# Spreading the reciprocal softmax sums over partitions: TensorE transposes against VectorE blocks and DRAM transfers

## The chip, the cores and the metric

The kernel runs on one core of one Trainium2 chip. The metric is the device time of one launch in microseconds (us); for each kernel it is the median of a few runs. Everything else in this text comes from one execution that the hardware profiler recorded.

A core has these engines: TensorE (in the profile PE for matmuls, PEld for the loads of their weights), VectorE (DVE), ScalarE (ACT), GpSimd (POOL), and SyncE (SP), which here only issues transfers. Each engine works through its own queue in order.

## The reference

Two layers of a hybrid decoder. Each layer takes 528 positions (16 learned meta tokens and 512 real ones) of width 1024. One projection feeds eight heads of attention with a forget gate and four heads of retention; their outputs go through one output projection, and a SwiGLU network follows. The part that the change touches is the softmax of the attention heads:

```python
def attend(q_blk, c_q, q_pos, k_, v_, c_k, k_pos):
    s = jnp.einsum('bhqd,bhkd->bhqk', q_blk, k_).astype(jnp.float32) * scale
    s = s + c_q[..., :, None] - c_k[..., None, :]
    s = jnp.where(k_pos[None, :] <= q_pos[:, None], s, -jnp.inf)
    p = jax.nn.softmax(s, axis=-1)
    return jnp.einsum('bhqk,bhkd->bhqd', p.astype(v_.dtype), v_)
```

Every query row is divided by the sum of its exponentials. All arithmetic is float32.

## The kernel before

Activations are kept transposed: features lie on the 128 partitions and positions along the free axis. Every matmul that matters is run three times, on a high and a low part of each operand (`split`: ScalarE casts the high part, VectorE subtracts it to get the low one).

Attention heads go in pairs: head pair g (0 to 3) holds heads 2g and 2g+1, called s = 0 and 1, of 64 features each. For each s and each block b of 128 queries the steps are:

- `scores(s, b)`: TensorE multiplies queries and keys (line 497), VectorE adds the mask to the diagonal (503) and the gates and takes the maximum (504), ScalarE takes the exponential and its sum over the keys (517). Queries lie on partitions here, so the sum is one column of 128 numbers.
- `turn(s, b)`, three steps later: TensorE transposes the unnormalised probabilities block by block (`transpose_into`, line 409), ScalarE and VectorE split them into `pth` and `ptl` (lines 137 and 138). The last 16 columns of all four blocks are transposed by VectorE in 32 by 32 blocks (line 521, tile `pe`).
- `product(s)`: TensorE multiplies values and probabilities (line 567); ScalarE copies one half of the result (570, tile `ol`) and VectorE adds the other (571). Features now lie on partitions and queries along the free axis.

The division is put off to the end of the pair. After the last `scores` the eight columns of sums (two heads, four blocks) are turned into reciprocals (line 525). ScalarE spreads each of them over 64 columns (527). In `product(1)` TensorE transposes the four 128 by 128 blocks so made (576), which leaves in PSUM, for each feature row, the reciprocal of its head and query, and VectorE multiplies the product of the pair by it (577). Then the pair is split (`mix_tile`) for the output projection, which comes much later for most pairs.

The four retention heads are worked on in the same stretch: `scores` (694, 699), `product` (724), `head_norm`, `gate`. They share ScalarE, VectorE and the four one-bank PSUM tiles (`psum_a`) with attention. Between these steps TensorE runs the dense projections (`dense_steps`, line 210), whose weights SyncE loads from DRAM (line 153, tile `raw`, three buffers), ScalarE casts (186) and, for most, GpSimd subtracts (187).

The order on TensorE is written out by hand: `merge` and `spread` place the steps between the chunks of the dense projections, and `manual_schedule` keeps that order. On the other engines a scheduler decides the order when the program is built, from its own estimates of durations. So an edit on one engine can move neighbouring instructions on others, although their lines are the same.

`tags` gives the tile `tq` a ring of four buffers (tag `w`) that several helpers share; the spread reciprocals take one of them.

Of the kernel before, what the change touches and what calls it, by code (L numbers as in the profile page):

```python
# [10 lines left out]
F32 = mybir.dt.float32  # L11
# [6 lines left out]
SEQ = 512  # L18
META = 16
T = SEQ + META  # L20
# [10 lines left out]
NBLK = SEQ // 128  # L31
# [8 lines left out]
def hybrid_kernel(ctx, tc, x_t, w_in, w_fl, w_out, w_gate, w_up, w_down, vecs, b_fg, rope, decay, mask, ident, out_t):  # L40
    nc = tc.nc

    const = ctx.enter_context(tc.tile_pool(name="const", bufs=1))
    state = ctx.enter_context(tc.tile_pool(name="state", bufs=1))
# [8 lines left out]
    idt = const.tile([128, 128], F32, name="idt")  # L53
# [10 lines left out]
    onec = const.tile([128, 1], F32, name="onec")  # L64
    nc.vector.memset(onec, 1.0)

    p_tiles, t_tiles, pm_tiles, v_tiles, end_tiles, low_keys = [], [], [], [], [], []
    rot = {"pm": 0}

# [182 lines left out]
    def psum_a():  # L252
        return psa.tile([128, 512], F32, name="psa", tag="psa")
# [5 lines left out]
    def tt(name, dt=F32):  # L259
        tag, bufs = tags[name]  # L260
        return tmp.tile([128, T], dt, name=name, tag=tag, bufs=bufs)
# [198 lines left out]
    def fox_steps(g, st, ly, real):  # L460

        blocks = list(range(0 if real else -1, NBLK))
        todo = [(s, b) for s in range(2) for b in blocks]
        info = {}

        def values():
            st["v"] = [at(f"vv{s}", shape=(128, 5, 128)) for s in range(2)]
            for j0, n, p3 in transpose_into(st["vt"], KOFF):
                for s in range(2):
                    v = st["v"][s][:, j0:j0 + n]  # L470
                    a0, a1 = ROWS[s]
                    b0, b1 = ROWS[1 - s]
                    nc.scalar.copy(v[:, :, a0:a1], p3[:, :, a0:a1])
                    nc.vector.tensor_sub(v[:, :, b0:b1], p3[:, :, a0:a1], v[:, :, a0:a1].bitcast(F32))
            st["mt"] = at("mixt", F32)

        def span(b):
            nq = META if b < 0 else 128
            nk = META if b < 0 else META + 128 * (b + 1)
            return nq, nk, (0 if b < 0 else META + 128 * b)  # L480

        def scores(s, b):
            nq, nk, q0 = span(b)
            if b == blocks[0]:
                bc = at("bc", F32, bufs=2)
                hd = 2 * g + s
                nc.sync.dma_start(bc, ly["cdr"][hd:hd + 1, :].partition_broadcast(128))
                st["bc"] = bc
            bc = st["bc"]
            segs = FULL if nk == T else ((0, nk),)  # L490
            pt = take(pm_tiles, "pm") if b < 0 else p_tiles[0][:, PSTEP * b:PSTEP * b + nk]
            mins = []
            normalise()
            for c0, c1 in segs:
                sc = psum_a()
                for i, kk in enumerate(st["k"][s]):
                    nc.tensor.matmul(sc[0:nq, 0:c1 - c0], st["q"][s][:, q0:q0 + nq], kk[:, c0:c1],  # L497
                                     start=(i == 0), stop=(i == 1))
                nm = tmp.tile([128, 1], F32, name="nmax", tag="nmax", bufs=6)
                with tc.high_priority():  # L500
                    if c1 == nk:
                        diag = sc[0:nq, c1 - c0 - nq:c1 - c0]
                        nc.vector.tensor_add(diag, diag, msk[0:nq, 0:nq])
                    nc.vector.tensor_tensor_reduce(pt[0:nq, c0:c1], sc[0:nq, 0:c1 - c0], bc[0:nq, c0:c1],  # L504
                                                   -1.0, 3.0e38, ALU.add, ALU.min, nm[0:nq])
                mins.append(nm)
            nmax = mins[0]
            if len(mins) > 1:
                nc.vector.tensor_tensor(nmax, mins[0], mins[1], ALU.min)
            if b < 0:  # L510
                rsum = tmp.tile([META, 1], F32, name="rsum", tag="rsum", bufs=4)
            else:
                if (s, b) == (0, 0):
                    st["sums"] = tmp.tile([128, NBLK, 2], F32, name="sums", tag="sums")
                rsum = st["sums"][:, b, s:s + 1]
            pr = pt[0:nq, 0:nk]
            nc.scalar.activation(pr, pr, AF.Exp, bias=nmax[0:nq], scale=-1.0, accum_out=rsum)  # L517
            info[s, b] = pt
            if b == blocks[-1]:
                st["ends"] = at("pe", F32, (32, NBLK, 32), 2)  # L520
                nc.vector.transpose(st["ends"], ends(p_tiles[0])[96:128])
            if b < 0:
                info["open"] = (pr, rsum)
            elif (s, b) == todo[-1]:
                nc.vector.reciprocal(st["sums"], st["sums"])
                st["rows"] = tt("tq")
                nc.scalar.copy(st["rows"][:, 0:SEQ].rearrange("p (b s d) -> p b s d", b=NBLK, s=2),
                               st["sums"].unsqueeze(3).broadcast_to([128, NBLK, 2, 64]))

        def normalise():  # L530
            if "open" in info:
                pr, rs = info.pop("open")
                nc.vector.reciprocal(rs, rs)
                nc.vector.tensor_scalar_mul(pr, pr, rs)

        def turn(s, b):
            nq, nk, q0 = span(b)
            pth, ptl = t_tiles
            if (s, b) == todo[-2]:
                normalise()  # L540
            if b < 0:
                e = at("pe", F32, (32, NBLK, 32), 2)[:, 0]
                nc.vector.transpose(e, info[s, b])
                split(pth[0:META, 0, 0:META], ptl[0:META, 0, 0:META], e[0:META, 0:META])
                return
            for j0, n, p3 in transpose_into(info[s, b], [128 * j for j in range(b + 1)]):
                split(pth[:, j0:j0 + n, q0:q0 + nq], ptl[:, j0:j0 + n, q0:q0 + nq], p3[:, :, 0:nq])
            if b == blocks[-1]:
                split(*[corners(t)[0:META, 1:] for t in (pth, ptl)], st["ends"][0:META, :, 32 - META:32])

        def product(s):
            mt, v, pt = st["mt"], st["v"][s], t_tiles
            a0, a1 = ROWS[s]
            b0, b1 = ROWS[1 - s]
            ol = tt("ol")
            if not real:
                po = psum_a()
                for i, pp in enumerate(pt):
                    nc.tensor.matmul(po[:, 0:META], v[:, 0, :], pp[:, 0, 0:META], start=(i == 0), stop=(i == 1))
                with tc.high_priority():  # L560
                    nc.scalar.copy(ol[a0:a1, 0:META], po[b0:b1, 0:META])
                    nc.vector.tensor_add(mt[a0:a1, 0:META], po[a0:a1, 0:META], ol[a0:a1, 0:META])
            po = psum_a()
            for j in range(5):
                c0 = max(0, KOFF[j] - META)
                for i, pp in enumerate(pt):
                    nc.tensor.matmul(po[:, c0:SEQ], v[:, j, :], pp[:, j, META + c0:T],  # L567
                                     start=(j == 0 and i == 0), stop=(j == 4 and i == 1))
            with tc.high_priority():
                nc.scalar.copy(ol[a0:a1, META:T], po[b0:b1, :])  # L570
                nc.vector.tensor_add(mt[a0:a1, META:T], po[a0:a1, :], ol[a0:a1, META:T])
            if s == 1:

                rb = psum_a()
                for b in range(NBLK):
                    nc.tensor.transpose(rb[:, 128 * b:128 * b + 128], st["rows"][:, 128 * b:128 * b + 128], idt)
                nc.vector.tensor_mul(mt[:, META:T], rb, mt[:, META:T])
                mh, ml = mix_tile(2 * (g % 2))
                split(sv(mh, real), sv(ml, real), sv(mt, real))
                st["mix"] = (mh, ml)  # L580

        steps = []
        n = len(todo)
        lag = 3
        for i in range(n + lag):
            if i < n:
                steps.append(lambda a=todo[i]: scores(*a))
            if i == 1:
                steps.append(values)
            if i >= lag:  # L590
                s, b = todo[i - lag]
                if s == 1 and b == blocks[0]:
                    steps.append(late(lambda: product(0)))
                steps.append(lambda a=(s, b): turn(*a))
        steps.append(lambda: product(1))
        cut = len(steps) - lag - 1
        return steps[:cut], steps[cut:]
# [627 lines left out]
    def layer(l):  # L1225

        real = l == DEPTH - 1
        QC = REAL if real else FULL
        ly, ff = {"wait": []}, {}
        fox = [{} for _ in range(FP)]  # L1230
        ret = [{} for _ in range(RH)]

# [170 lines left out]
```

## Time and profile before

| what | value |
|---|---|
| time, median of 3 runs | 1278.95 us (1278.76 to 1279.9) |
| time of the profiled execution | 1278.89 us |
| its span from the first to the last instruction | 1277.1 us |
| mean granted TensorE clock | 0.996 of full speed |
| PE busy | 1258.0 us, 99% |
| DVE busy | 1019.4 us, 80% |
| ACT busy | 687.7 us, 54% |
| POOL busy | 181.0 us, 14% |

The profiled execution is 1.8 us longer than its span, and 0.06 us from the median. In rows of a timeline the first number is the start and the second the duration, both in us; a bracket gives the idle time before it and what ended it. In rows of the chain of waits the same two numbers stand before the engine and line. A query on one line gives the shortest, median and longest duration in ns.

### The profile page before, as it was taken

To read this page: it belongs to the slowest core of one execution; us is meant where nothing else is said; L and a number is where in the kernel's file an instruction comes from. 1 tells how busy PE (TensorE), PEld (TensorE's weight loads), DVE (VectorE), ACT (ScalarE), POOL (GpSimd) and SP (SyncE) were. 2 spreads that over 40 slices of the span, in tenths; PEclk is the share of its full clock that TensorE was granted. 3 is DMA by queue.
4 is the path that set the end of the run, shared out by engine and by line. 5 is a ranking of instruction groups with operands and counts; after the bars stand their busy time and mean duration, and the time that the engine had idled before them with its cause. 6 is when DMAs were issued, how large, how long until landed. Compare 5 with 4: busy or idle time off the path is not lost.

```text
span 1277.1 us, 23190 instructions
## 1 busy us (share of the span) xinstructions
PE 1258.0 (99%) x9265; PEld 1197.8 (94%) x9265; DVE 1019.4 (80%) x1849; ACT 687.7 (54%) x1250; POOL 181.0 (14%) x150
## 2 busy tenths in 40 slices
PE   9999999999999999999999999999999999999997
PEld 8899999999999999999999989999789999999996
DVE  7888866879988888887687878568899878888867
ACT  7566655576544444444455665456764444444445
POOL 2233333210000000000014334332000000000001
PEclk9999999999999999999999999999999999999998
DMA  6222222223323333332323122222223333333321
GB/s 233 76 67 84 75 84 84 66 73 115 107 97 100 100 100 100 100 100 83 100 76 112 65 100 84 77 91 66 100 83 130 102 100 100 100 100 100 103 79 67
DMA packets 45677, 120.55 MB, mean 94 GB/s; under 512 B 5360, under 2 KB 12272, under 8 KB 45568
## 3 DMA queue, kind: packets, MB, share of 16 engines
q1 hardware_dynamic: 45136, 118.77, 28.4%
q8 instruction: 73, 1.20, 0.4%
q10 hardware_dynamic: 432, 0.29, 0.1%
q14 instruction: 36, 0.29, 0.1%
HBM read 116.91 MB, written 2.13 MB: 93 GB/s over the span
## 4 chain that ended last, share of the span: by engine, by line
PE 84%; DVE 10%; ACT 4%; DMA 1%; issue 1%; DVEq 0%; POOL 0%; ACTq 0%
PE psd L210 24%; PE psa L875 18%; PE psd L1010 14%; PE psd L875 13%; PE psa L1010 4%; PE psa L210 3%; PE psa L409 2%; PE psa L497 1%; PE psa L567 1%; PE psa L724 1%; PE psa L694 1%; DVE qs L429 1%; DMA bc<-cdr 1%; DVE pr L504 1%; DVE rsl L138 0%
## 5 line engine op out<-in xcount | busy, mean ns | idle before, releaser
L187 POOL TENSOR_TENSOR wlo<-raw,whi 128x512 fp32r<-128x512 f32 x126 | 172.3, 1381 | 380.2 <-ACT whi L186 380.2
L210 PE MATMUL psd<-xh,whi 128*128 128x264 f32 (+1 forms) x792 | 195.8, 315 | 0.0
L210 PE MATMUL psd<-xl,whi 128*128 128x264 f32 (+1 forms) x792 | 186.5, 303 | 0.6 <-DVE xl L313 0.6
L210 PE MATMUL psd<-xh,wlo 128*128 128x264 f32 (+1 forms) x792 | 186.9, 303 | 0.0
L210 PEld LDWEIGHTS psd<-xh,whi 128*128 128x128 f32 x792 | 128.7, 190 | 4.7 <-ACT whi L186 0.4
L210 PEld LDWEIGHTS psd<-xh,wlo 128*128 128x128 f32 x792 | 127.2, 188 | 6.2 <-DVE wlo L187 0.4
L210 PEld LDWEIGHTS psd<-xl,whi 128*128 128x128 f32 x792 | 128.0, 189 | 5.2 <-DVE xl L313 1.2
L186 ACT CAST whi<-raw 128x512 fp32r<-128x512 f32 (+1 forms) x168 | 98.3, 613 | 39.2 <-PE psd L210 19.9
L863 ACT CAST whi<-raw 128x1024 fp32r<-128x1024 f32 (+2 forms) x62 | 54.9, 885 | 51.3 <-PE psd L875 39.9
L863 ACT CAST fwhi<-raw 128x1024 fp32r<-128x1024 f32 (+2 forms) x62 | 55.6, 897 | 48.1 <-PE psd L875 40.5
L864 DVE TENSOR_TENSOR wlo<-raw,whi 128x1024 fp32r<-128x1024 f32 (+2 forms) x62 | 62.9, 1014 | 13.7 <-ACT whi L863 13.6
L864 DVE TENSOR_TENSOR fwlo<-raw,fwhi 128x1024 fp32r<-128x1024 f32 (+2 forms) x62 | 64.0, 1032 | 10.8 <-ACT fwhi L863 10.5
L875 PE MATMUL psa<-th,whi 128*128 128x264 f32 (+1 forms) x232 | 65.4, 282 | 0.0
L875 PE MATMUL psa<-th,wlo 128*128 128x264 f32 (+1 forms) x232 | 65.4, 282 | 0.0
L875 PE MATMUL psa<-tl,whi 128*128 128x264 f32 (+1 forms) x232 | 65.3, 282 | 0.0
L875 PE MATMUL psa<-th,fwhi 128*128 128x264 f32 (+1 forms) x224 | 63.4, 283 | 0.0
L875 PE MATMUL psa<-tl,fwhi 128*128 128x264 f32 (+1 forms) x224 | 63.3, 283 | 0.0
L875 PE MATMUL psa<-th,fwlo 128*128 128x264 f32 (+1 forms) x224 | 63.3, 282 | 0.0
L517 ACT ACTIVATE pr<-pr,nmax 128x144 f32<-128x144 f32 (+1 forms) x64 | 36.9, 576 | 42.8 <-DVE nmax L504 30.5
L941 ACT COPY e<-psa 128x264 f32<-128x264 f32 (+1 forms) x114 | 42.9, 376 | 27.9 <-PE psa L875 23.6
L863 ACT CAST fwhi<-S 128x1024 fp32r<-128x1024 f32 x20 | 21.0, 1049 | 68.6 <-PE psa L875 66.5
L1010 PE MATMUL psd<-ah,fwlo 128*128 128x264 f32 (+1 forms) x200 | 56.6, 330 | 0.0
(355 smaller groups left out, 4008.6 us busy)
## 6 DMA issues: line engine op xcount, KB each, us to landing
raw<-w_in SPq DMA_DIRECT2D x54, 512.0 KB, 3.5
raw<-w_gate SPq DMA_DIRECT2D x44, 512.0 KB, 4.0
fraw<-w_up SPq DMA_DIRECT2D x38, 512.0 KB, 3.4
raw<-w_down SPq DMA_DIRECT2D x64, 256.0 KB, 2.7
raw<-w_out SPq DMA_DIRECT2D x16, 512.0 KB, 3.5
raw<-w_down SPq DMA_DIRECT2D x32, 192.0 KB, 2.5
bc<-cdr SPq DMA_DIRECT2D x16, 264.0 KB, 3.3
raw<-w_up SPq DMA_DIRECT2D x6, 512.0 KB, 3.5
```

The source lines that it names most:

```text
L186: pin(nc.scalar.copy(hi, job["raw"][:, c0:c1]), pinned)
L187: pin(sub(lo, job["raw"][:, c0:c1], hi.bitcast(F32)), pinned)
L210: nc.tensor.matmul(ps[1][b][:, 0:c1 - c0], w[:, wk, :], x[:, c0:c1], start=(k == 0 and i == 0), stop=(k == n - 1 and i == 2))
L409: nc.tensor.transpose(ps[:, 128 * j:128 * j + 128], src[:, o:o + 128], idt)
L429: nc.vector.tensor_sub(sv(t, real, b0, b1), sv(tq, real, a0, a1), sv(t, real, a0, a1).bitcast(F32))
L497: nc.tensor.matmul(sc[0:nq, 0:c1 - c0], st["q"][s][:, q0:q0 + nq], kk[:, c0:c1], start=(i == 0), stop=(i == 1))
L517: nc.scalar.activation(pr, pr, AF.Exp, bias=nmax[0:nq], scale=-1.0, accum_out=rsum)
L863: nc.scalar.copy(hi, src)
L864: nc.vector.tensor_sub(lo, src, hi.bitcast(F32))
L875: nc.tensor.matmul(bank()[:, 0:b.shape[-1]], a[:, o + k, :], b, start=(fresh and k == 0 and i == 0), stop=(k == n - 1 and i == 2), skip_gr ...
L941: nc.scalar.copy(self.t["e"][:, i], self.t["x"][:, 0:w])
L1010: nc.tensor.matmul(v[:, 0:c1 - c0], a[:, s * n + k, :], b[:, c0:c1], start=(k == 0 and i == 0), stop=(k == n - 1 and i == 2))
```

## The change

The sums of a pair go into a fixed tile of 32 columns (two such tiles take turns), zeroed once. When all eight columns are there, VectorE takes the reciprocals and turns the tile in 32 by 32 blocks. Four small transfers write the eight useful rows of each block to DRAM, as eight rows of 128 numbers; two transfers read them back, each as one row of 512 numbers copied to 64 partitions. The last product of the pair reads this tile in SBUF in place of the one in PSUM. ScalarE's spreading copy and TensorE's four transposes are gone. The reciprocal and the turning are marked as of high priority for the scheduler. Lines below the second hunk have numbers higher by up to 9 in the changed kernel than in the diff's left side (577 becomes 582).

```diff
+    sum_tiles = [state.tile([128, 32], F32, name=f"sums{i}") for i in range(2)]
+    for t in sum_tiles:
+        nc.gpsimd.memset(t, 0.0)
...
             else:
-                if (s, b) == (0, 0):
-                    st["sums"] = tmp.tile([128, NBLK, 2], F32, name="sums", tag="sums")
-                rsum = st["sums"][:, b, s:s + 1]
+                rsum = sum_tiles[g % 2][:, NBLK * s + b:NBLK * s + b + 1]
...
             elif (s, b) == todo[-1]:
-                nc.vector.reciprocal(st["sums"], st["sums"])
-                st["rows"] = tt("tq")
-                nc.scalar.copy(st["rows"][:, 0:SEQ].rearrange("p (b s d) -> p b s d", b=NBLK, s=2),
-                               st["sums"].unsqueeze(3).broadcast_to([128, NBLK, 2, 64]))
+                sums = sum_tiles[g % 2]
+                turned = tmp.tile([128, 32], F32, name="turned", tag="turned")
+                with tc.high_priority():
+                    nc.vector.reciprocal(sums[:, 0:2 * NBLK], sums[:, 0:2 * NBLK])
+                    nc.vector.transpose(turned, sums)
+                rdr = tc.dram_tile([2 * NBLK, 128], F32, name=f"rdr{ly['l']}{g}")
+                for a in range(4):
+                    nc.sync.dma_start(rdr[:, 32 * a:32 * a + 32], turned[32 * a:32 * a + 2 * NBLK, :])
+                st["rows"] = tt("tq")[:, 0:SEQ]
+                wide = rdr.rearrange("(s b) q -> s (b q)", s=2)
+                for i, (a0, a1) in enumerate(ROWS):
+                    nc.sync.dma_start(st["rows"][a0:a1], wide[i:i + 1, :].partition_broadcast(64))
...
             if s == 1:
-
-                rb = psum_a()
-                for b in range(NBLK):
-                    nc.tensor.transpose(rb[:, 128 * b:128 * b + 128], st["rows"][:, 128 * b:128 * b + 128], idt)
-                nc.vector.tensor_mul(mt[:, META:T], rb, mt[:, META:T])
+                nc.vector.tensor_mul(mt[:, META:T], st["rows"], mt[:, META:T])
...
-        ly, ff = {"wait": []}, {}
+        ly, ff = {"wait": [], "l": l}, {}
```

## The prediction

> **What bounds the kernel now.** I read the page first: busy time per engine, then the chain that ended last.
>
> ```profile
> PE 1258.0 (99%) x9265; PEld 1197.8 (94%) x9265; DVE 1019.4 (80%) x1849; ACT 687.7 (54%) x1250; POOL 181.0 (14%) x150
> ...
> PE 84%; DVE 10%; ACT 4%; DMA 1%; issue 1%; DVEq 0%; POOL 0%; ACTq 0%
> ```
>
> TensorE is busy 99% of the span and carries 84% of the chain: time taken from it is time saved, if the work that feeds it keeps its places. The other 16% says that this isn't so everywhere. The timeline of TensorE, read for its idle time, shows where:
>
> ```profile
> 95.41 0.78 PE L409 MATMUL psa<-idt,pd 128*128 128x128 f32 x4 [0.88 <-DVE pd L449]
> 157.60 0.51 PE L210 MATMUL psd<-mxh,whi 128*128 128x264 f32 x2 [0.90 <-DVE h L778]
> ```
>
> Here TensorE waits 0.88 and 0.90 us for VectorE: in layer 0's first two pairs VectorE sets the end, and a TensorE saving is lost there. All times below are in us; each of the eight pairs (four a layer, g0 to g3) is costed by itself, since each has other neighbours.
>
> **What goes from TensorE.** The chain of waits around the removed transposes of one pair, and the group of the removed copies:
>
> ```profile
> 177.33 1.56 PE psd L210 x12
> ...
> 190.83 0.51 PE psa L576 x4
> 191.34 4.37 PE psd L210 x36
> ```
>
> ```profile
> L527 ACT COPY tq<-sums x8: 619/620/631, 67.7 to 873.6; 128x512 f32<-128x512 f32 x8
> ```
>
> The four transposes take 0.51. Twelve projection matmuls take 1.56 in the first row (it follows a product) and 4.37/3 = 1.46 in the row behind the transposes: what follows a product starts some 0.10 slower, and the transposes bear that now. So a pair saves 0.51 − 0.10 = 0.41 on TensorE, all eight at most 3.3. ScalarE loses eight copies of 0.62; it is 54% busy, so by itself this is worth nothing. What it does to the order comes below.
>
> **What is added, and whether it arrives in time.**
>
> ```profile
> 41.47 0.19 DVE L543 STREAM_TRANSPOSE pe<-pm 32x32 f32<-32x32 f32 x1
> 182.06 0.20 DVE L525 RECIPROCAL sums<-sums 128x8 f32<-128x8 f32 x1
> 193.15 0.69 DVE L577 TENSOR_TENSOR mixt<-psa,mixt 128x512 f32<-128x512 f32 x1
> ```
>
> ```profile
> bc<-cdr SPq DMA_DIRECT2D x16, 264.0 KB, 3.3
> ```
>
> ```profile
> 34.57 1.48 DMA cdr<-z
> ...
> 673.99 3.03 DMA cdr<-z
> ```
>
> The turn of 128x32 has no row; the nearest is a 32x32 turn of 0.19, and I take 0.2 (bounds 0.19 and 0.69, the multiply of 16 times the columns). The copy to rows in DRAM and back already occurs once a layer for the gates: `cdr` is written in 1.48 or 3.03, and its broadcast lands in 3.3. From the reciprocal: 0.4 on VectorE, four stores issued one after the other (estimate 0.4 each, half of the next row), 1.5 to 3.0 to land, two broadcasts issued, 3.3 to land:
>
> ```profile
> 36.06 0.81 SPq L487 DMA_DIRECT2D bc<-cdr  x2
> ```
>
> 0.4 + 1.6 + (1.5 to 3.0) + 0.8 + 3.3 = 7.6 to 9.1. The multiply comes 193.15 − 182.06 = 11.1 after the reciprocal in the tightest pair (layer 0, g2). So the rows arrive 2 to 3.5 before they are needed, and I charge nothing. SyncE's queue is passed by six transfers a pair; in six pairs the builder put one weight load between the stores and the broadcasts, which then starts some 2 early or late, with three `raw` buffers as cover: zero. If that cover fails, one late load of 512 KB costs at most the broadcasts' wait, about 3. The two memsets run before anything needs them.
>
> **What moves: the order on ScalarE and VectorE.** This is the large term. The changed program, as built, keeps TensorE's order but for the transposes, while around each place the scheduler has put ScalarE's and VectorE's neighbours in another order. In those stretches TensorE alternates between attention and retention, and both engines hand it operands with little slack. I followed the new order through the rows of before, pair by pair.
>
> *Layer 0, g0.*
>
> ```profile
> 69.95 0.49 PE L409 MATMUL psa<-idt,pr 128*128 128x128 f32 x3
> 70.32 0.71 DVE L138 TENSOR_TENSOR rsl<-sd,rsh 128x528 fp32r<-128x528 f32 x1 [0.73 <-ACT rsh L137]
> 71.24 0.40 PE L724 MATMUL psa<-rsl,rvh 128*128 128x512 f32 x1
> 71.98 0.48 ACT L137 CAST pth<-psa 128x384 fp32r<-128x384 f32 x1
> 73.40 0.59 ACT L137 CAST pth<-psa 128x512 fp32r<-128x512 f32 x1 [0.87 <-PE psa L409]
> ```
>
> `rsl` ends at 71.03 and TensorE uses it at 71.24. As built, the `pth` cast of 128x384 stands ahead of `rsh` on ScalarE: it waits for the transposes (69.95 + 0.49 = 70.44), takes 0.48, then `rsh` 0.6 and `rsl` 0.71 end at about 72.2. TensorE waits some 0.95, its next transposes come later, and the cast at 73.40, which waits for them, heads the VectorE stretch that ends at 95.41. Nothing is saved: +0.9 (0 to +1.8, as ScalarE's lost copy may pull the work ahead forward).
>
> *Layer 0, g1.* The removed copy was on this stretch's chain, but other products now wait behind a split; both orders meet again at
>
> ```profile
> 133.58 2.53 POOL L187 TENSOR_TENSOR wlo<-raw,whi 128x512 fp32r<-128x512 f32 x2 [3.97 <-ACT whi L186]
> 135.13 1.43 DVE L138 TENSOR_TENSOR rsl<-sd,rsh 128x416 fp32r<-128x416 f32 x1
> ```
>
> ```profile
> 891.73 0.59 DVE L138 TENSOR_TENSOR rsl<-sd,rsh 128x416 fp32r<-128x416 f32 x1
> ```
>
> where a subtraction that takes 0.59 elsewhere takes 1.43 beside GpSimd. I take 0 (−0.6 to +0.8).
>
> *Layer 0, g3.*
>
> ```profile
> 251.23 1.20 DVE L699 TENSOR_TENSOR sd<-psa,dec 128x264 f32<-128x264 f32 x3
> 252.55 0.39 PE L409 MATMUL psa<-idt,pr 128*128 128x128 f32 x2
> 253.50 0.71 PE L409 MATMUL psa<-idt,pd 128*128 128x128 f32 x5
> 254.54 0.41 DVE L138 TENSOR_TENSOR ptl<-psa,pth 128x256 fp32r<-128x256 f32 x1
> 254.88 0.87 DVE L662 TENSOR_REDUCE mean<-psa 128x4 f32<-128x512 f32 x2
> ```
>
> Now `sd` is made at 251.23, ahead of the split `ptl`. As built, `ptl` (which waits for 252.55 + 0.39 and a cast of some 0.36, and so ends at about 253.75) and the first mean (about 0.65 of the two's 0.87) stand ahead of it, so the first `sd` comes at 255.4. The fifth transpose of the 253.50 group needs it at about 253.95. TensorE waits 1.5; less 0.41: +1.1.
>
> *Layer 1, g0.*
>
> ```profile
> 703.34 0.58 ACT L570 COPY ol<-psa 64x512 f32<-64x512 f32 x1
> 703.95 0.68 DVE L571 TENSOR_TENSOR mixt<-psa,ol 64x512 f32<-64x512 f32 x1 [0.40 <-ACT ol L570]
> ...
> 707.84 0.61 ACT L137 CAST rsh<-sd 128x512 fp32r<-128x512 f32 x1
> 708.35 0.63 ACT L639 ACTIVATE gr<-gr 128x512 f32<-128x512 f32 x1
> 708.48 0.69 DVE L138 TENSOR_TENSOR rsl<-sd,rsh 128x512 fp32r<-128x512 f32 x1 [0.71 <-ACT rsh L137]
> ...
> 709.09 0.57 DVE L699 TENSOR_TENSOR sd<-psa,dec 128x400 f32<-128x400 f32 x1
> 709.23 0.50 PE L724 MATMUL psa<-rsl,rvh 128*128 128x512 f32 x1
> ```
>
> As built, `gr` (0.63) and `ol` (0.58) stand ahead of `rsh`, which then comes near 709; line 571 (0.68) and `sd` (0.57) stand ahead of `rsl`. That ends near 710.7 in place of 709.17, and TensorE wants it at 709.23: a wait of 1.4 in a stretch where VectorE leads until 722, so the 0.41 is lost too: +1.4.
>
> *Layer 1, g3.*
>
> ```profile
> 874.84 0.69 DVE L699 TENSOR_TENSOR sd<-psa,dec 128x512 f32<-128x512 f32 x1 [0.59 <-PE psa L694]
> 875.89 0.21 PE L567 MATMUL psa<-pth,vv 128*128 128x16 f32 x1
> 885.59 0.68 DVE L138 TENSOR_TENSOR ptl<-psa,pth 128x512 fp32r<-128x512 f32 x1
> 886.42 0.40 PE L567 MATMUL psa<-ptl,vv 128*128 128x512 f32 x1
> ```
>
> As built, the small split of `pe` stands ahead of `sd` on VectorE, and its cast overwrites what the product still reads until 875.89 + 0.21 = 876.1. `sd` comes near 876.4 in place of 874.84. VectorE is packed from there to `ptl`, which ends at 886.27, 0.15 before TensorE takes it: 1.56 − 0.15 − 0.41 = +1.0 (up to +1.7).
>
> *The other three* (layer 0 g2, layer 1 g1 and g2) get no new wait that I can find: −0.4 each.
>
> Sum: 0.9 + 0 + 1.1 + 1.4 + 1.0 − 3 × 0.4 = +3.2. The profiled execution took 1278.9, within 0.1 of the median, so the forecast is 1278.9 + 3.2 = 1282.1, slower. What a measurement of this kernel can tell from no change is about 0.2%, 2.6: the forecast lies just outside it.
>
> **The rivals.** *Gain only.* The new orders cost nothing, because ScalarE's eight freed copies move the work ahead of each place early enough. For it: ScalarE has 46% idle. Against: each of the four waits above is for TensorE's own results or for VectorE, not for ScalarE's time. Five to eight pairs at 0.41: 1275.6 to 1276.8, faster.
>
> *Half of the waits.* Some of the four are refilled from slack further on, as TensorE's queue holds weights loaded ahead. Two of the four leave 1.0 to 2.5 less: 1279.5 to 1281, no difference that counts.
>
> *Lock at the multiply.* The last multiply reads SBUF twice now, no longer PSUM. The rows at 133.58 and 135.13 show such an operation stretched by 0.84 beside GpSimd, and by up to GpSimd's remaining time. In the three pairs led by VectorE (layer 0 g0 and g1, layer 1 g0) a GpSimd operation that has slid under the multiply would add up to 1 each, +2.9 on the sum: 1285. It decides only where the two overlap, so only if a late place pushes the one under the other. [...]
>
> *Rows late.* If stores or broadcasts take over 2 more than the rows of `cdr` say, VectorE stands at the multiply, and behind it the split of the mixture, the key and query evictions and so TensorE. It counts from 11.1 in the tightest pair. With 2 late in four pairs: 1282 + 6 = 1288, slower.
>
> **How the numbers follow.** Forecast (most waits come, with or without a lock or two) 0.50; rows late 0.05; half of the waits 0.27; gain only 0.18. So slower 0.55, same 0.27, faster 0.18. The bounds of the four waits (0 to 1.8, and so on) give the forecast's own range of 1281.5 to 1285.5. The whole range takes in half of the gain cases below and the lock above: 1275.9 to 1286.5.
>
> **What would show it.** Right: TensorE idle ahead of L724 in layer 0 g0 and layer 1 g0 (about 0.9 and 1.4, ended by `rsl`), ahead of the transposes of `pd` in layer 0 g3 (ended by `sd`), and ahead of the last product of layer 1 g3; none in the other pairs; the multiply on VectorE at once behind line 571, near 0.69, with the broadcast landed 2 or more before. Wrong: no such idle time (then gain only), or idle time ahead of the multiply ended by a DMA (rows late), or a multiply of over 1 us (lock).

## The result and the profile after

| kernel | median | range of the runs |
|---|---|---|
| before | 1278.97 us | 1278.07 to 1279.9, 6 runs |
| changed | 1283.97 us | 1282.05 to 1285.76, 6 runs |

The ratio is 1.0043, with a 95% interval from 1.0033 to 1.0053: slower by 4.2 to 6.8 us. The profiled execution of the changed kernel took 1282.05 us (span 1280.2). In eight of the twelve profiled executions in this text the granted clock is halved for 3.4 us between 59 and 65 us, which adds some 1.5 us (1.44 by the first starts of TensorE compared further down; in that of `keep_transposes` a second time, at 893 us). The profiled execution of before has this and that of the changed kernel has not, so where traces are laid side by side below, only what comes behind 66 us is compared. A median can hold more or fewer of such executions, so a difference of under 1.5 us between two medians says little by itself. One execution of `order_of_before`, 1709.03 us at a granted clock of 0.668, and one of before beside it, 1353.88 us at 0.849, are left out of the ratios and of the median of `order_of_before` below.

The page of the changed kernel, its busy times and the chain that ended last:

```profile
PE 1255.9 (98%) x9233; PEld 1194.2 (93%) x9233; DVE 1021.8 (80%) x1857; ACT 684.3 (53%) x1242; POOL 181.4 (14%) x152
...
PE 81%; DVE 11%; ACT 5%; DMA 2%; issue 1%; DVEq 0%; ACTq 0%; SPq 0%
```

TensorE is busy 2.1 us less (up to 1.5 of it the clock), and its share of the chain has gone from 84% to 81%: more of the chain is waiting for others. The view of TensorE's waits says for whom. Its columns are the waiting line, the releaser, the sum in us, the count and the longest. Before, these were among the largest entries (`pd` is the wait quoted in the prediction):

```profile
PE psa L567 <- DVE ptl L138: 1.7, 1, 1.7
...
PE psd L210 <- DVE h L778: 0.9, 1, 0.9
PE psa L409 <- DVE pd L449: 0.9, 1, 0.9
```

The changed kernel has these, new or longer:

```profile
PE psa L576 <- DVE ptl L141: 3.8, 2, 2.0
...
PE psa L412 <- DVE pd L452: 1.1, 1, 1.1
PE psa L412 <- DVE sd L704: 1.1, 1, 1.1
...
PE psa L729 <- DVE rsl L141: 0.9, 2, 0.7
...
PE psa L729 <- ACT rsh L140: 0.4, 1, 0.4
```

A second wait for `ptl` of 2.0, one for `sd`, two for `rsl`, one for `rsh`: these are the operands that the prediction followed. No entry names a DMA.

The new operations themselves (a query on each new line, then on the transfers):

```profile
L530 DVE STREAM_TRANSPOSE turned<-sums x8: 211/212/213, 66.1 to 874.3; 128x32 f32<-128x32 f32 x8
L582 DVE TENSOR_TENSOR mixt<-tq,mixt x8: 691/693/695, 80.6 to 892.4; 128x512 f32<-128x512 f32 x8
```

```profile
DMA to landing us min/median/max: 2.8/3.4/4.3
```

```profile
181.67 0.19 DVE L529 RECIPROCAL sums<-sums 128x8 f32<-128x8 f32 x1
...
185.88 0.59 SPq L537 DMA_DIRECT2D tq<-rdr  x1
193.20 0.69 DVE L582 TENSOR_TENSOR mixt<-tq,mixt 128x512 f32<-128x512 f32 x1
```

The turn takes 0.21, the multiply 0.69 in all eight places, as with its PSUM operand, and the broadcasts land a median of 3.4 after their issue. In the tightest pair the second one is issued at 185.88 and so lands at about 189.3 (an estimate from that median; the trace has no landing for this one); the multiply comes at 193.20, and no bracket behind it shows a wait.

### The profile page after: what moved, and what is told of

Read it like the earlier page. It is cut to its first block, busy times and chain, and to the rows that moved or that the text cites. A ratio compares the mean times of both kernels' runs of the same rounds, so it can differ in the third digit from the quotient of the medians.

```text
span 1280.2 us, 23201 instructions
## 1 busy us (share of the span) xinstructions
PE 1255.9 (98%) x9233; PEld 1194.2 (93%) x9233; DVE 1021.8 (80%) x1857; ACT 684.3 (53%) x1242; POOL 181.4 (14%) x152
## 4 chain that ended last, share of the span: by engine, by line
PE 81%; DVE 11%; ACT 5%; DMA 2%; issue 1%; DVEq 0%; ACTq 0%; SPq 0%
PE psd L213 22%; PE psa L880 18%; PE psd L1015 14%; PE psd L880 13%; PE psa L1015 4%; PE psa L213 4%; PE psa L412 1%; PE psa L500 1%; PE psa L576 1%; PE psa L729 1%; PE psa L699 1%; DVE ptl L141 1%; DVE pr L507 1%; ACT whi L189 1%; DVE tq L618 1%
```

## The experiments

Theory A: the time was lost by the new order of ScalarE and VectorE around each pair; the transfers, the turn and the multiply cost nothing. Theory B: it came with the transfers. ScalarE's and VectorE's order can be held by edges (`how` below) that order two instructions of one engine without a wait between them; `PINS` stands for lists of such instructions, by their places in program order (`by` holds each engine's instructions in that order), for the stretches around the eight pairs.

All runs, each against runs of the kernel before on the same chip (1278.6 to 1278.8 us median):

| kernel | median us | ratio to before, 95% interval |
|---|---|---|
| order_of_before | 1277.62 | 0.9994 [0.9985, 1.0003] |
| before_order_of_after | 1286.00 | 1.0064 [1.0052, 1.0077] |
| no_transposes | 1276.55 | 0.9983 [0.9974, 0.9992] |
| keep_transposes | 1286.22 | 1.0061 [1.0049, 1.0073] |
| no_trip | 1277.43 | 0.9991 [0.9982, 1.0] |
| two_places | 1279.81 | 1.0009 [1.0, 1.0018] |
| best_order | 1274.47 | 0.9971 [0.9959, 0.9982] |
| keep_copy | 1276.19 | 0.9987 [0.9979, 0.9996] |
| before_moves | 1276.35 | 0.9985 [0.9977, 0.9994] |
| two_hops | 1274.71 | 0.9975 [0.9965, 0.9985] |

**The order alone, both ways.** `order_of_before` is the changed kernel with the old order:

```diff
+    for eng, runs in PINS.items():          # the order of before, on ScalarE and VectorE
+        for c in runs:
+            for a, b in zip(c, c[1:]):
+                tc.add_manual_dep(by[eng][b], by[eng][a].name, how, reason="order")
     enter(None)
```

> The changed kernel with every instruction of ScalarE and VectorE held in the order of the kernel before (each turn right behind its reciprocal); TensorE's transposes and ScalarE's copies stay away, the transfers stay. Theory A (the cost of the change is the new order of the two engines): the four long waits go, 0.41 us a pair is saved in the pairs led by TensorE, VectorE's extra turns of 0.2 us take a little back in the three pairs led by it: 1276.8 us, between 1275.7 and 1277.8. Theory B (the cost comes with the transfers: contention, late rows, or the multiply's second SBUF operand): it stays at 1283 to 1285 us.

`before_order_of_after` has the same lines in the kernel before, with the changed kernel's order in `PINS`.

> The kernel before, with its transposes and copies and without any transfer of the sums, its ScalarE and VectorE instructions held in the order that the changed kernel has (each copy behind the instruction it stood behind). Theory A: all waits of the changed kernel come, without its saving on TensorE: 1285.5 us, between 1284 and 1287. Theory B: no more than 1280 us, as nothing of the transfers is there.

Both came out as A has it. 1277.62 against 1283.97: the order of before takes the whole loss away although every transfer is there. 1286.00 against 1278.7: the order of the changed kernel makes the kernel before 7 us slower although no transfer of the sums is there. TensorE's waits in the trace of `before_order_of_after` are the changed kernel's new ones, one by one (beside a shorter one for `ptl` at 130 us that the changed kernel doesn't have):

```profile
PE psa L567 <- DVE ptl L138: 3.8, 2, 2.0
...
PE psa L409 <- DVE sd L699: 1.1, 1, 1.1
PE psa L724 <- DVE rsl L138: 1.0, 2, 0.7
...
PE psa L724 <- ACT rsh L137: 0.4, 1, 0.4
```

`order_of_before` lay 0.8 us above its expected time, within its range; rows below say why.

**TensorE's part alone.** `no_transposes`:

```diff
-                rb = psum_a()
-                for b in range(NBLK):
-                    nc.tensor.transpose(rb[:, 128 * b:128 * b + 128], st["rows"][:, 128 * b:128 * b + 128], idt)
-                nc.vector.tensor_mul(mt[:, META:T], rb, mt[:, META:T])
+                nc.vector.tensor_mul(mt[:, META:T], st["rows"][:, 0:SEQ], mt[:, META:T])
```

> The kernel before without its 32 transposes of the spread reciprocals; the last multiply reads ScalarE's copy as it stands (the division is by the wrong query's sum), and nothing else is changed. This is TensorE's saving alone. Theory A: 0.41 us in five to eight pairs: 1275.7 to 1276.9 us. Theory B says the same of this one. If the transposes were hidden under other waits: 1278 to 1279 us.

`keep_transposes` gives the changed kernel four transposes a pair back:

```diff
+                rb = psum_a()
+                for b in range(NBLK):
+                    nc.tensor.transpose(rb[:, 128 * b:128 * b + 128], idt, idt)
                 nc.vector.tensor_mul(mt[:, META:T], st["rows"], mt[:, META:T])
```

> The changed kernel with four transposes a pair given back to TensorE at their old place (of the identity, read by nobody). Theory A: the saving of five to eight pairs goes, the waits stay: 1286 to 1287.3 us. If TensorE's saving was lost behind the waits: 1284 to 1285 us.

Without them the kernel before gains 2.2 us by the medians (1.0 to 3.3), and 3.2 behind 66 us in the trace. With them the changed kernel loses 2.25 more by the medians. Laid matmul by matmul beside the changed kernel, the four transposes cost 0.41 in each of the eight pairs, 3.3 in all, and 1.1 comes back in layer 0 g0, where VectorE's `ge` is again ahead of GpSimd's subtraction and takes 0.70 (the changed kernel's two rows stand further down, under layer 0 g0):

```profile
86.29 0.70 DVE L757 SCALAR_TENSOR_TENSOR ge<-ge,gr 128x528 f32<-128x528 f32 x1
...
86.58 1.56 POOL L190 TENSOR_TENSOR wlo<-raw,whi 128x512 fp32r<-128x512 f32 x1 [5.46 <-ACT whi L189]
```

The saving is as large as foretold, and it isn't what went wrong in the sum; but in that one place it brings a loss of its own.

**What was left in `order_of_before`.** `no_trip` is `order_of_before` with rows that are there early:

```diff
-                rdr = tc.dram_tile([2 * NBLK, 128], F32, name=f"rdr{ly['l']}{g}")
-                for a in range(4):
-                    nc.sync.dma_start(rdr[:, 32 * a:32 * a + 32], turned[32 * a:32 * a + 2 * NBLK, :])
                 st["rows"] = tt("tq")[:, 0:SEQ]
-                wide = rdr.rearrange("(s b) q -> s (b q)", s=2)
+                wide = ly["cdr"]
                 for i, (a0, a1) in enumerate(ROWS):
-                    nc.sync.dma_start(st["rows"][a0:a1], wide[i:i + 1, :].partition_broadcast(64))
+                    nc.sync.dma_start(st["rows"][a0:a1], wide[i:i + 1, 0:SEQ].partition_broadcast(64))
```

> order_of_before without the four stores of a pair; its two broadcasts read a row of the gates in DRAM, which is there long before (the division is by wrong numbers). The rows are early now, and 32 small transfers are gone; reciprocal, turn, the multiply from SBUF and the order of ScalarE and VectorE stay. order_of_before took 1277.8 us, 1.2 us more than no_transposes. Theory A (the transfers cost nothing; the 1.2 us is a lock between VectorE and GpSimd at line 754 in layer 0's first pair, 0.7 to 1.8 us, and a wait of 0.4 us for rsl in layer 0 g3): 1277.8 us within 0.7. Theory B (the 1.2 us is the price of the transfers or of late rows): 1276.6 us.

1277.43 is 0.2 from `order_of_before` and nearer to A. The 1.1 us that `order_of_before` has over `no_transposes` by the medians (2.1 behind 66 us in the traces) begins in these rows of its trace:

```profile
84.75 1.29 POOL L190 TENSOR_TENSOR wlo<-raw,whi 128x512 fp32r<-128x512 f32 x1 [5.11 <-ACT whi L189]
84.81 1.80 DVE L754 SCALAR_TENSOR_TENSOR ge<-ge,gr 128x528 f32<-128x528 f32 x1
...
265.39 0.39 PE L729 MATMUL psa<-rsl,rvh 128*128 128x272 f32 x1 [0.36 <-DVE rsl L141]
```

Before, the same two operations stood the other way round:

```profile
84.84 0.70 DVE L749 SCALAR_TENSOR_TENSOR ge<-ge,gr 128x528 f32<-128x528 f32 x1
85.15 1.55 POOL L187 TENSOR_TENSOR wlo<-raw,whi 128x512 fp32r<-128x512 f32 x1 [5.55 <-ACT whi L186]
```

GpSimd's subtraction waits for ScalarE's cast, and before that cast ScalarE waited 0.26 for TensorE's projection matmuls (84.45 in the trace of before). TensorE is 0.4 earlier by its saving, so GpSimd now starts 0.06 before VectorE, and VectorE takes 1.80 in place of 0.70, in a stretch that VectorE leads. Beside `no_transposes` TensorE comes 0.8 later there. The two pairs of rows show `ge` at 1.80 where GpSimd starts 0.06 ahead of it and at 0.70 where GpSimd starts 0.31 behind it; that a lock does this, as theory A has it, isn't shown. The last row is a wait of 0.36 for `rsl`, which the transposes had covered; the matmuls behind it start 0.6 later, and the same wait comes again in layer 1 g3. Some 0.4 is given back in layer 1 g0, and a slow drift, of which more below, makes up the rest.

**One place at a time.** `two_places` keeps in `PINS` only the stretches of the last pair of each layer.

> The changed kernel with ScalarE and VectorE held in the order of the kernel before in two of the eight places alone, the last pair (g3) of each layer. Theory A, by the trace of the changed kernel: TensorE's waits of 1.7 us in layer 0 g3 and of 2.4 us in layer 1 g3 go, the others stay: 1284.0 - 4.1 = 1279.9 us, between 1279 and 1281. Rival (the places hang together, and a wait taken out of one is given back in the next): 1282 us or more.

1279.81: a difference of 4.2 us by the medians against 4.1 read from the trace, which looks like a hit. The traces say less. Both long waits are gone, each with nearly the size that was read, but the view of waits has two more for `rsl`, one in each g3:

```profile
PE psa L729 <- DVE rsl L141: 1.6, 4, 0.7
```

They are those of `order_of_before`. Each costs 0.6, and TensorE comes out 3.0 ahead of the changed kernel behind 66 us. So nothing is given back in the other places, as A has it, but that the medians gave 4.2 is partly luck.

**A smaller edit.** `keep_copy` does without `PINS`:

```diff
                 st["rows"] = tt("tq")[:, 0:SEQ]
+                nc.scalar.copy(st["rows"].rearrange("p (b s d) -> p b s d", b=NBLK, s=2),
+                               sums[:, 0:2 * NBLK].rearrange("p (s b) -> p b s", s=2).unsqueeze(3).broadcast_to([128, NBLK, 2, 64]))
```

> The changed kernel with ScalarE's eight copies back: they write the row tile, which the broadcasts then overwrite, so they do nothing but stand in the scheduler's way. By the order in which it is built the four long waits are gone. Theory A: as order_of_before, without the wait of 0.4 us for rsl in layer 0 g3: 1277.4 us, between 1276.5 and 1278.3. Theory B: 1284 us, as the transfers are the same.

1276.19, a little under the expected range. As built, its order is that of before but for the reciprocals, the turns and the tails of both g3. So the thing that had moved the neighbours was chiefly the removal of ScalarE's copy, and a copy that nobody reads makes the change a gain.

**The best order.** `best_order` is `order_of_before` with these moves in `PINS` (and without the edge that kept `ge` behind the split of `sq`):

```
 VectorE, four places:   mxl, sql, ge, gr        ->  mxl, ge, sql, gr
 VectorE, g3 of both:    mxl (mixture), rsl      ->  rsl, mxl (mixture)
```

> order_of_before with two moves on VectorE: line 754 (ge) goes ahead of the split of sq in the four places, into a gap of 1.1 us in which VectorE waits for ScalarE, and in both layers' g3 the split rsl (and its cast rsh) goes ahead of that of the mixture, as in the changed kernel. Theory A: ge no longer meets GpSimd's subtraction in layer 0 g0 (1.1 us, all of TensorE's idle time there), 0.7 us less in layer 0 g1, 0.4 us in layer 0 g3, 0.3 us in layer 1 g0: 1277.8 - 2.5 = 1275.3 us, between 1274.5 and 1276.5. If gr, the next one, is locked in place of ge: 1276.5 to 1277.5 us.

`before_moves` has the same moves in the kernel before.

> The kernel before, with its transposes and copies, and the two moves of best_order (ge ahead of the split of sq in four places, rsl ahead of the split of the mixture in both layers' g3). It parts what the moves give from what the change gives in the same order. Theory A: ge's move gives up to 0.9 us in layer 0 g0 (TensorE's idle time there), nothing elsewhere, and rsl's move nothing, as the transposes still cover that wait: 1278.8 - 0.8 = 1278.0 us, between 1277.3 and 1278.8; best_order, the same order with the change, took 1274.5, so the change is worth some 3.3 us when no order stands in its way. Rival (the moves alone give best_order's gain): 1275.5 us or less.

`best_order` took 1274.47, faster than before by 0.2 to 0.4%. `ge` runs early, and GpSimd now meets the next one. Against the kernel before that costs nothing more, as `gr` took 1.68 there too; against `before_moves`, where `gr` takes 0.70, TensorE loses 0.7 here:

```profile
81.76 0.70 DVE L754 SCALAR_TENSOR_TENSOR ge<-ge,gr 128x528 f32<-128x528 f32 x1
...
83.53 3.01 POOL L190 TENSOR_TENSOR wlo<-raw,whi 128x512 fp32r<-128x512 f32 x2 [5.11 <-ACT whi L189]
83.59 1.80 DVE L755 SCALAR_TENSOR_TENSOR gr<-ge,gr 128x528 f32<-128x528 f32 x1
```

`before_moves` missed: 1276.35 where 1277.3 to 1278.8 was expected. Its profiled execution took 1276.35 too, and that of before 1278.89, 2.5 more. Of this 1.5 is the halved clock, which the trace of before has and that of `before_moves` has not. Laid matmul by matmul behind 66 us, the moves gain 0.8 at the transposes of `pd` (95.41 before), as expected, and 0.3 in all that follows: 1.1 in all, so the 2.2 between the medians flatters them. The trace of `best_order` has no halved clock either, and lies 2.5 ahead of that of `before_moves` behind 66 us (their spans are 1.9 apart). So the change in a good order is worth 1.9 to 2.5 us, less than the 3.3 expected, and 0.7 of what is missing is lost at `gr`.

**Where late rows begin.** `two_hops` is `best_order` with the rows two DRAM copies later:

```diff
+                for hop in range(2):
+                    nxt = tc.dram_tile([2 * NBLK, 128], F32, name=f"hop{hop}{ly['l']}{g}")
+                    nc.sync.dma_start(nxt, rdr)
+                    rdr = nxt
                 wide = rdr.rearrange("(s b) q -> s (b q)", s=2)
```

> best_order with the reciprocals copied twice more from DRAM to DRAM between the stores and the broadcasts, so that the rows come later by two issues and two landings, about 5 us by the rows of the first trip. By the trace of the changed kernel the rows land some 3.3 us before the multiply in layer 0 g2, 4.5 in g1, 6 to 7 in the others. Theory A (rows cost only where they are later than the multiply): VectorE waits about 2 us in layer 0 g2 and under 1 in g1, for which TensorE pays in part: 1274.5 + 1 to 2.5, so 1275.5 to 1277 us. Theory B (every transfer costs, early or late): 1280 us or more.

The multiply now waits for its rows in three pairs of layer 0, and the trace shows it as the prediction's rival would have looked:

```profile
138.60 0.69 DVE L586 TENSOR_TENSOR mixt<-tq,mixt 128x512 f32<-128x512 f32 x1 [0.81 <-DMA tq<-hop]
194.42 0.69 DVE L586 TENSOR_TENSOR mixt<-tq,mixt 128x512 f32<-128x512 f32 x1 [1.24 <-DMA tq<-hop]
260.88 0.69 DVE L586 TENSOR_TENSOR mixt<-tq,mixt 128x512 f32<-128x512 f32 x1 [0.24 <-DMA tq<-hop]
```

VectorE waits 2.3 us in all, and the time is 1274.71, 0.24 above `best_order` and below the expected range. TensorE loses 0.3 at 141 us and has it back at 156: what stands behind the multiply is split for a projection that comes much later. Late rows were a cheap danger here, even two hops late.

## Why the prediction was right, and where its steps were off

The forecast was 1282.1, slower, and the time is 1284.0: the sign and the mechanism were right, and the sum of +3.2 was too small. To see each step, the start of every matmul was compared with that of the same matmul before. One example: the transposes at 69.95 and the product at 71.24 before are these in the changed kernel,

```profile
68.51 0.49 PE L412 MATMUL psa<-idt,pr 128*128 128x128 f32 x3
...
70.09 0.49 PE L729 MATMUL psa<-rsh,rvh 128*128 128x512 f32 x1 [0.36 <-ACT rsh L140]
70.84 0.50 PE L729 MATMUL psa<-rsl,rvh 128*128 128x512 f32 x1 [0.25 <-DVE rsl L141]
```

so the lead of 1.44 (the clock) shrinks to 0.40: this place cost 1.0. The changes over each pair, in us:

| pair | forecast | measured | made of |
|---|---|---|---|
| layer 0 g0 | +0.9 | +1.7 | waits 1.0, saving -0.4, longer `ge` +1.1 |
| layer 0 g1 | 0 | -0.3 | saving -0.4, small waits 0.1 |
| layer 0 g2 | -0.4 | -0.3 | saving -0.4, small waits 0.1 |
| layer 0 g3 | +1.1 | +1.4 | waits 1.8, saving -0.4 |
| layer 1 g0 | +1.4 | +0.5 | wait 0.6, saving -0.4, given back 0.3 |
| layer 1 g1 | -0.4 | 0 | wait 0.4, saving -0.4 |
| layer 1 g2 | -0.4 | -0.4 | saving |
| layer 1 g3 | +1.0 | +2.1 | wait 2.5, saving -0.4 |
| sum | +3.2 | +4.7 | |

Over the whole stretch behind 66 us TensorE falls back by 4.5 (its lag is how much later a matmul starts than the same one before). The difference is made between the pairs and behind the last: 0.2 of the waits comes back behind each g3, and in the long dense stretches TensorE's lag falls by 0.4 from 300 to 640 us and grows by 0.6 from 900 to 1250. `order_of_before`, `best_order` and `no_trip`, all built from the changed kernel, drift there alike; `no_transposes`, `before_moves` and `before_order_of_after`, built from the one before, don't. Nothing of the edit runs there, and no run says where this drift comes from.

Of the four pairs that the forecast charged, three are off by 0.8 to 1.1, in both directions. That the sum came as near as it did is partly luck.

*The saving.* 0.41 at the place of the transposes in every pair, as forecast; also in the pairs led by VectorE, where the prediction had it lost at once. There it was saved first, and in layer 1 g0 given back later.

*Rows in time.* Right: 185.88 + 3.4 − 181.67 = 7.6 after the reciprocal in the tightest pair (with the median landing), at the lower end of 7.6 to 9.1.

*Layer 0 g3.* Right to 0.3. The forecast had the fifth transpose of `pd` waiting for the first `sd`; here the first four wait too, for `ptl`:

```profile
253.10 0.42 DVE L141 TENSOR_TENSOR ptl<-psa,pth 128x256 fp32r<-128x256 f32 x1 [1.14 <-ACT pth L140]
253.58 0.66 PE L412 MATMUL psa<-idt,pd 128*128 128x128 f32 x4 [0.19 <-DVE ptl L141]
...
254.27 0.69 DVE L667 TENSOR_REDUCE mean<-psa 128x4 f32<-128x512 f32 x1 [0.75 <-PE psa L412]
...
254.88 0.42 DVE L704 TENSOR_TENSOR sd<-psa,dec 128x264 f32<-128x264 f32 x1
255.36 0.33 PE L412 MATMUL psa<-idt,pd 128*128 128x128 f32 x1 [1.12 <-DVE sd L704]
```

The working of this step doesn't add up, though. Its terms give 253.75 + 0.65 + 0.40 (a third of the row of three `sd`) = 254.8 for the first `sd`, and not 255.4. The trace has a term that the forecast didn't write down, a wait of the mean for TensorE, 0.75 in the rows above; that 255.4 met the measured 255.30 owes something to luck.

*Layer 0 g0.* The wait was right (1.0, forecast 0.95). "Nothing is saved" failed, and so did the place that the rival "Lock at the multiply" gave: it isn't the new multiply (at 80.55, where it takes 0.69) that takes longer beside GpSimd but `ge`, almost 4 us behind it (1.80 in place of 0.70), and the saving itself brings GpSimd there. Runs show this: with the new order but without the saving, in `before_order_of_after` and `keep_transposes`, GpSimd starts 0.3 behind `ge`, which then takes 0.70. `no_transposes`, with the saving in the order of before, starts both at 84.88, and `ge` takes 0.70 there too: the saving brings the two level, and what made the last 0.06 isn't shown.

```profile
84.34 3.00 POOL L190 TENSOR_TENSOR wlo<-raw,whi 128x512 fp32r<-128x512 f32 x2 [5.11 <-ACT whi L189]
84.40 1.80 DVE L754 SCALAR_TENSOR_TENSOR ge<-ge,gr 128x528 f32<-128x528 f32 x1
```

*Layer 1 g0.* Too large by 0.9. The step charged line 571 (0.68) at its new place ahead of `rsl` but didn't credit that it had left its old one: `sg`, behind it before, starts at 703.79 and `gr` at 707.30, each 1 us earlier than before. (ScalarE's `ol`, which the step moved too, and its spreading copy, 0.58 and 0.62, had left that place as well; no run parts them from line 571.)

```profile
703.79 0.68 DVE L632 SCALAR_TENSOR_TENSOR sg<-psd,R 128x512 f32<-128x512 f32 x1
...
707.30 0.63 ACT L644 ACTIVATE gr<-gr 128x512 f32<-128x512 f32 x1
...
710.39 0.50 PE L729 MATMUL psa<-rsl,rvh 128*128 128x512 f32 x1 [0.69 <-DVE rsl L141]
```

*Layer 1 g1 and g3.* Too small. In both a small split, moved by the new order, starts while GpSimd is running and takes five to seven times as long: 1.32 where it took 0.20 before, and 1.26 where a split of the same size at 761.69 takes 0.27. That the wait of 0.4 in g1, which the forecast hadn't found, comes from this is read from the order of the rows and wasn't tested.

```profile
758.96 2.73 POOL L190 TENSOR_TENSOR wlo<-raw,whi 128x512 fp32r<-128x512 f32 x2 [2.62 <-ACT whi L189]
760.45 1.32 DVE L141 TENSOR_TENSOR ptl<-pe,pth 16x64 fp32r<-16x64 f32 x1
...
762.47 0.20 DVE L138 TENSOR_TENSOR ptl<-pe,pth 16x64 fp32r<-16x64 f32 x1
```

```profile
877.42 0.67 DVE L704 TENSOR_TENSOR sd<-psa,dec 128x512 f32<-128x512 f32 x1
...
886.93 2.54 POOL L190 TENSOR_TENSOR wlo<-raw,whi 128x512 fp32r<-128x512 f32 x2 [2.62 <-ACT whi L189]
887.08 1.26 DVE L141 TENSOR_TENSOR rvl<-sq,rvh 128x128 fp32r<-128x128 f32 x1 [0.25 <-ACT rvh L140]
...
889.46 0.50 PE L576 MATMUL psa<-ptl,vv 128*128 128x512 f32 x1 [2.03 <-DVE ptl L141]
```

(The last row of the first fence is from the trace of before.) The delay of `sd` in g3 was right in kind: 877.42 − 874.84 = 2.58, of which 0.7 is how late TensorE came there.

*The rivals.* "Gain only" (1275.6 to 1276.8) didn't come as built, but comes near what the change does once the order is held or ScalarE's copy is back: 1277.6 and 1276.2. "Half of the waits" didn't come: all four did, one of them at less than half its size. "Rows late" was refuted, and `two_hops` shows it to be cheap. "Lock at the multiply" was right that a VectorE operation takes longer beside GpSimd (`ge`, 1.80 in place of 0.70) and had the wrong instruction: the multiply takes 0.69 in all eight places. That a lock is behind the longer times was the author's reading; no run shows what is.

## What to carry to other kernels

Where a scheduler orders the engines, compare the built order before and after an edit, and follow each moved instruction through the rows of before: here the saving, the turn, the multiply and the landing of the rows came out within 0.1 us of their estimates and the neighbours' order made the sign. When an instruction leaves a place, credit its old place as well as charging its new one. And when one engine becomes faster, ask which pair of VectorE and GpSimd operations changes sides: where GpSimd started 0.06 us ahead of VectorE, one operation took 1.80 us in place of 0.70.

## What the runs showed of the hardware

The halved clock between 59 and 65 us wasn't expected. The windows of TensorE in the trace of before, and in that of the changed kernel (length, busy and count, granted clock, DMA share, GB/s):

```profile
50.00:60.00 10.00, 8.25 (x65) 1.00 0.26 77
60.00:66.00 6.00, 6.00 (x39) 0.72 0.29 91
```

```profile
50.00:60.00 10.00, 8.19 (x65) 1.00 0.22 78
60.00:66.00 6.00, 6.00 (x52) 1.00 0.29 89
```

The same work, busy for the same 82% just before, is followed by a drop in one execution and by none in the other. The drop is to half clock (windows of 1 us in the trace of before have 0.50 from 61 to 64 us), for (1 - 0.72) × 6.00 / 0.5 = 3.4 us. Why it comes in some executions only, and why for 3.4 us, no run here shows.
